# Hybrid encoder trunk on one core: low-part score matmul over 128 rows with zero-padded key tiles, five temporaries in place of six

## The chip, the cores and the metric

The kernel runs on one core of a Trainium2 chip. The time is the device time of one execution, in microseconds (us), and a kernel's figure is the median of its runs. TensorE does the matmuls (PE; its weight loads are PEld), VectorE (DVE), ScalarE (ACT) and GpSimd (POOL) the elementwise work, and SyncE (SP) issues most of the DMAs.

## The reference, cut to what matters

Two layers work on one sequence of 512 tokens with 1024 channels, all in float32. Each layer is half a SwiGLU step, four attention mixers side by side with four heads of 64 channels each, a projection back, another half SwiGLU step and a gate; an RMSNorm stands before each. The mixers are a neighbourhood attention (NA), a sliding window (SWA), a dilated window (DIL) and a latent one (MLA).

```python
for i in range(DEPTH):
    x = x + 0.5 * swiglu(rms_norm(x, ffn1_norm[i]), ffn1_w_gate[i], ffn1_w_up[i], ffn1_w_down[i])
    z = rms_norm(x, mix_norm[i]) @ w_in[i]
    z_na, z_swa, z_dil, z_mla = jnp.split(z, IN_SPLITS, axis=-1)
    y = jnp.concatenate([rms_norm(y_m, group_norm[i, m]) for the four mixers], axis=-1)
    x = x + y @ w_out[i]
    x = x + 0.5 * swiglu(rms_norm(x, ffn2_norm[i]), ffn2_w_gate[i], ffn2_w_up[i], ffn2_w_down[i])
    gate = jax.nn.sigmoid(rms_norm(x, ple_norm[i]) @ ple_w_gate[i])
    x = x + gate * (p[i] @ ple_w_proj[i])
return rms_norm(x, final_norm)
# in every mixer, for one head and a block of 128 queries:
#   s = q @ k.T * scale (+ bias, or masked);  o = softmax(s) @ v
```

## The kernel before, in words

**Products of two parts.** Activations lie in SBUF with channels on the 128 partitions and the 512 tokens in the free dimension. A float32 operand is kept as a high part (its rounding to the matmul's format) and a low part (what is left), and a product is three matmuls: high by high, high by low, low by high. For the projections these are L200, L201 and L202 in `mm3y`, each 128 rows by 512 columns. The weights come in by DMA (`pieces`, L157 to L175): a tile of raw weights lands, ScalarE rounds it into `wh`, and VectorE subtracts to make `wl` (GpSimd does it in the attention part, where `mixing` is set).

**Keys and queries.** Two heads share a tile: the first has rows 0 to 63, the second 64 to 127. `stack` (L333 to L350) prepares such a tile for the score product. Of the keys it makes a tile `t` with one half for each head, in which the head's 64 rows hold the high part and the other 64 rows a copy of it, and a tile `kl` [128, 512] whose rows hold the low parts of both heads, each in its own 64 rows (L341 to L343; the tag `kl` has two buffers). Of the queries it makes one tile with a half for each head: the head's own rows hold the high part, the other 64 rows the low part. So one matmul of 128 rows (L397) gives high by high plus low by high, and a second one (L398) over the head's 64 rows alone adds high by low:

```python
nc.tensor.matmul(s, lhsT=q[:, e, qs], rhs=k[0][:, e, k0:k1], start=True, stop=False)
nc.tensor.matmul(s, lhsT=q[rows, e, qs], rhs=k[1][rows, k0:k1], start=False, stop=True)
```

This holds for NA, SWA and DIL. The latent heads have 96 channels, and `rows` is None there: three matmuls of 128 rows (L392 to L394).

**One head.** `qk` runs for four blocks of 128 queries. A block's scores `s` have 256 or 384 columns where the window is a band, 512 otherwise. L404 on VectorE adds the mask and takes the minimum (or L401 without a mask), ScalarE takes the exponential into a tile `P` (L410; eight buffers). `tr` transposes P on TensorE (L439, into a score bank), ScalarE and VectorE split it into `PT` (L442, L443), and `pv` multiplies it with the values (L455, twice for each block, high and low); L463 adds two halves of that bank. After each second head `pair_end` spreads the softmax factors by transposes (L469). `value` scales a projection (L363 or, permuted, L361) and transposes it later (L368).

**The order of the work.** In `mix` a loop goes over 16 heads and six steps for each; at a step it issues score, transpose and pv work of the heads that are under way, and then `pump` issues a share of the projections of the later heads, so that TensorE has work while the other engines do the softmax. TensorE's instructions and SP's DMAs run in the order in which the program is written. The order on VectorE, ScalarE and GpSimd comes from the framework's scheduler, which also hands out the buffers. `mix` starts with the NA heads, then SWA, the latent ones, DIL.

**Temporaries.** `tmp` (L56) is a ring of six tiles of 128x512 float32. It serves the rotation (L326, L328, L330), the sums of squares (L215 on ScalarE, L216 on GpSimd), the gate blocks of the feed-forward part (`gated`, two tiles for each of the 88 blocks: L273 empties the gate bank into one, tanh goes to the other, L276 and L277 multiply, L120 makes the split), and the latent heads (`d_lat`, `d_kpe`, `d_up`). At the start of the latent heads `d_lstat` makes the factor `rkv` of the latent's norm, in a tile of its own (L558, by `rspread`, L239), and `d_up` uses it for keys (L586) and values (L363); a copy of the rotary key goes into each latent key tile (a DMA issued by GpSimd), after the split of the rotary key (L122 and L120).

`setup_mix` (L98) loads the masks for the attention part; it is called in the first feed-forward part.

Of the kernel before, what the change touches and what calls it, by code (L numbers as in the profile page):

```python
# [9 lines left out]
F32 = mybir.dt.float32  # L10
F32R = mybir.dt.float32r
AF = mybir.ActivationFunctionType
ALU = mybir.AluOpType
# [4 lines left out]
T = 512  # L18
# [16 lines left out]
class Encoder:  # L35
# [18 lines left out]
        return self.sb.tile(shape, dt, tag=tag, name=self.nm(tag), bufs=bufs)  # L54

    def tmp(self):  # L56
        return self.tile("tmp", [128, T], F32, 6)

    def act(self):
        return self.tile(self.tags[0], [128, 2, T], F32R, 8)  # L60
# [37 lines left out]
    def setup_mix(self):  # L98
        nc, a, c = self.nc, self.a, self.const
        self.sink = c.tile([128, self.depth, 4], F32, name="sink")  # L100
        nc.sync.dma_start(self.sink, a["sink"])
        self.nsink = c.tile([128, self.depth, 4], F32, name="nsink")
        nc.gpsimd.tensor_scalar(out=self.nsink, in0=self.sink, scalar1=-1.0, scalar2=None, op0=ALU.mult)
        self.na_mask = c.tile([128, 7, 16], F32, name="na_mask")
        nc.sync.dma_start(self.na_mask, a["na_mask"])
        self.swa_mask = c.tile([128, 384], F32, name="swa_mask")
        nc.sync.dma_start(self.swa_mask, a["swa_mask"])
        self.dil_mask = c.tile([128, 896], F32, name="dil_mask")
        nc.sync.dma_start(self.dil_mask, a["dil_mask"])

    def g(self, l, off, k):
        c = l * GAINS + off + k
        return self.gain[:, c:c + 1]
# [122 lines left out]
            nc.tensor.transpose(bc[:, t * 128:(t + 1) * 128], rc[:, t:t + 1].to_broadcast([128, 128]), self.ident)  # L236
        return bc

    def rspread(self, rc, tag="rb"):  # L239
        nc = self.nc  # L240
        bc = self.spread(rc)
        rb = self.tile(tag, [128, T], F32, 1)
        nc.scalar.activation(rb, bc, AF.Copy)
        return rb

# [87 lines left out]
    def stack(self, u, scale):  # L333
        nc = self.nc
        t = self.big()
        lo, up = slice(0, 64), slice(64, 128)
        if scale is None:
            for e, r, w in ((0, lo, up), (1, up, lo)):
                nc.scalar.activation(t[r, e], u[r], AF.Copy)
                nc.vector.tensor_copy(t[w, e], t[r, e].bitcast(F32))  # L340
            kl = self.tile("kl", [128, T], F32R, 2)  # L341
            for e, r in ((0, lo), (1, up)):
                nc.vector.tensor_tensor(out=kl[r], in0=u[r], in1=t[r, e].bitcast(F32), op=ALU.subtract)  # L343
            return t, kl
        for e, r in ((0, lo), (1, up)):
            nc.scalar.activation(t[r, e], u[r], AF.Copy, scale=scale)
        for e, r, w in ((0, lo, up), (1, up, lo)):
            nc.vector.scalar_tensor_tensor(out=t[w, e], in0=u[r], scalar=scale, in1=t[r, e].bitcast(F32),
                                           op0=ALU.mult, op1=ALU.subtract)
        return t  # L350
# [28 lines left out]
    def qk(self, st, t):  # L379
        nc, h = self.nc, st  # L380
        band, mask, sink = h["band"], h["mask"], h["sink"]
        if t == 0:
            h["ne"] = self.tile("ne", [128, 4], F32, 3)
            h["P"], h["k0"] = [], []
        q, k, rows, ne = h["q"], h["k"], h["rows"], h["ne"]
        k0 = 128 * max(0, t - 1) if band else 0
        k1 = 128 * min(4, t + 2) if band else T
        w = k1 - k0
        s = self.small()[:, :w]
        qs = slice(t * 128, (t + 1) * 128)  # L390
        if rows is None:
            nc.tensor.matmul(s, lhsT=q[:, 0, qs], rhs=k[:, 0, k0:k1], start=True, stop=False)  # L392
            nc.tensor.matmul(s, lhsT=q[:, 0, qs], rhs=k[:, 1, k0:k1], start=False, stop=False)
            nc.tensor.matmul(s, lhsT=q[:, 1, qs], rhs=k[:, 0, k0:k1], start=False, stop=True)  # L394
        else:
            e = h["odd"]
            nc.tensor.matmul(s, lhsT=q[:, e, qs], rhs=k[0][:, e, k0:k1], start=True, stop=False)  # L397
            nc.tensor.matmul(s, lhsT=q[rows, e, qs], rhs=k[1][rows, k0:k1], start=False, stop=True)  # L398
        p = self.tile("P", [128, T], F32, 8)
        if mask is None:  # L400
            nc.vector.tensor_reduce(ne[:, t:t + 1], s, AX.X, ALU.min)  # L401
            src = s
        else:
            nc.vector.tensor_tensor_reduce(  # L404
                out=p[:, :w], in0=s, in1=mask(t), scale=1.0,
                scalar=3e38 if sink is None else sink[0], op0=ALU.add, op1=ALU.min,
                accum_out=ne[:, t:t + 1])
            src = p[:, :w]
        ls = h["l8"][:, h["odd"]]
        nc.scalar.activation(p[:, :w], src, AF.Exp, bias=ne[:, t:t + 1], scale=-1.0,  # L410
                             accum_out=ls[:, t:t + 1])
        h["P"].append(p)
        h["k0"].append(k0)
        if t == 3:
            if sink is not None:
                se = self.tile("se", [128, 4], F32, 2)
                nc.scalar.activation(se, ne, AF.Exp, bias=sink[1])
                nc.vector.tensor_tensor(ls, ls, se, op=ALU.add)
            if h["odd"]:
                rl = self.tile("rl", [128, 2, 4], F32, 2)  # L420
                nc.vector.reciprocal(rl, h["l8"])
                rx = self.tmp()
                nc.scalar.activation(rx.rearrange("p (t e d) -> p t e d", t=4, e=2),
                                     rl.rearrange("p e t -> p t e").unsqueeze(3).to_broadcast([128, 4, 2, 64]),
                                     AF.Copy)
                h["rx"] = rx
# [125 lines left out]
    def d_lstat(self):  # L552
        nc, a = self.nc, self.a
        yield

        def finish():
            r = self.rspread(self.t["rq"], "rg")
            self.rkv = self.rspread(self.t["rkv"], "rkv")  # L558
            t = self.tile("nb", [128, 896], F32, 1)[:, :T]
            nc.sync.dma_start(t, a["mlaq"])  # L560
            nc.gpsimd.tensor_tensor(out=t, in0=t, in1=r, op=ALU.mult)
            self.mlaq = t

        self.later.append([7, finish, "lstat"])
        return True
# [414 lines left out]
```

## Time and profile before

| | |
|---|---|
| runs | 2168.96 us median of 3 (2166.63, 2168.96, 2170.75) |
| profiled execution: span | 2163.3 us; no whole time of its own is given, so the median stands 5.66 us above this span |
| TensorE busy | 2117.2 us, 98% (9564 matmuls); weight loads 1718.6 us |
| VectorE busy | 1210.5 us, 56% |
| ScalarE busy | 930.1 us, 43% |
| GpSimd busy | 280.0 us, 13% |
| mean granted clock of TensorE | 0.994 of full speed |

The span is the time from the profiled execution's first to its last instruction. Busy time is the sum over an engine's instructions, overlaps taken once; a matmul's row begins before the one ahead of it is through, so the durations of neighbouring rows add up to more than the time they take, and the step from one start to the next is what one costs. A wait is an idle stretch, with the instruction that ended it. The two layers take turns with two tile tags (`act` and `big`): what is named big in the first layer is named act in the second, so the same line has two groups. The attention part of the first layer lies between 395 and 640 us, that of the second between about 1460 and 1705.

### The profile page before, as it was taken

Reading aid. Unit: us, or ns where it says so; the run is one execution under the profiler, and the core shown is the slowest. Engines: PE = TensorE matmul, PEld = TensorE weight load, DVE = VectorE, ACT = ScalarE, POOL = GpSimd, SP = SyncE. Lnnn points to the kernel's source line nnn. Section 1 sums busy time; section 2 is a strip of 40 time slices with the busy share of each in tenths; the row PEclk is TensorE's granted clock in tenths of the full one; section 3 lists DMA queues with packets and bytes.
Section 4 is the critical chain, followed back from the end, with each engine's and each line's share of the span. In section 5 each row is a group of like instructions: output and inputs, shape, how many; then the busy total and the mean of one; then the engine's idle time right before and its main releaser. Section 6 shows DMA issues by size and latency. Waiting matters only on the chain.

```text
span 2163.3 us, 25721 instructions
## 1 busy us (share of the span) xinstructions
PE 2117.2 (98%) x9564; PEld 1718.6 (79%) x9564; DVE 1210.5 (56%) x1926; ACT 930.1 (43%) x1690; POOL 280.0 (13%) x230
## 2 busy tenths in 40 slices
PE   8999999999999999999999999999999999999997
PEld 6888888677778888888888888886777788888886
DVE  5444446567766444456654444555687654444554
ACT  4332334477754332333533233345677533233343
POOL 2000001444321000001100000025332200000011
PEclk9999999999999999999999999999999999999998
DMA  3232223212112222223322322232121122322322
GB/s 129 97 109 99 98 94 111 90 60 75 40 54 93 98 96 99 98 98 96 100 96 98 94 102 98 93 102 93 64 59 49 59 98 98 94 101 98 102 92 89
DMA packets 63358, 195.38 MB, mean 90 GB/s; under 512 B 7552, under 2 KB 15872, under 8 KB 63232
## 3 DMA queue, kind: packets, MB, share of 16 engines
q1 hardware_dynamic: 61808, 187.92, 26.0%
q0 software_dynamic: 1280, 5.77, 1.0%
q8 instruction: 75, 1.23, 0.2%
q14 instruction: 51, 0.42, 0.1%
q10 hardware_dynamic: 144, 0.05, 0.0%
HBM read 189.51 MB, written 2.10 MB: 89 GB/s over the span
## 4 chain that ended last, share of the span: by engine, by line
PE 92%; DVE 4%; ACT 2%; issue 1%; DMA 1%; POOL 0%; POOLq 0%; SPq 0%; DVEq 0%; ACTq 0%
PE ps L200 15%; PE ps L201 15%; PE ps L202 15%; PE s L201 13%; PE s L200 13%; PE s L202 13%; PE pv L455 2%; PE s L439 2%; PE s L398 2%; PE s L397 1%; DVE kl L343 1%; PE s L225 1%; PE s L236 0%; ACT tmp L326 0%; DVE PT L443 0%
## 5 line engine op out<-in xcount | busy, mean ns | idle before, releaser
L173 ACT ACTIVATE wh<-raw 128x512 fp32r<-128x512 f32 (+1 forms) x712 | 437.8, 615 | 971.2 <-PE ps L201 457.3
L175 DVE TENSOR_TENSOR wl<-raw,wh 128x512 fp32r<-128x512 f32 (+1 forms) x614 | 435.6, 710 | 405.6 <-ACT wh L173 399.0
L200 PE MATMUL ps<-act,wh 128*128 128x512 f32 x616 | 248.8, 404 | 6.1 <-ACT act L122 6.1
L216 POOL TENSOR_TENSOR acc<-acc,tmp 128x512 f32<-128x512 f32 x54 | 72.3, 1340 | 1365.4 <-ACT tmp L215 1365.0
L200 PE MATMUL ps<-big,wh 128*128 128x512 f32 x616 | 247.0, 401 | 0.0
L201 PE MATMUL ps<-act,wh 128*128 128x512 f32 x616 | 242.7, 394 | 3.3 <-DVE act L123 3.1
L202 PE MATMUL ps<-act,wl 128*128 128x512 f32 x616 | 242.1, 393 | 0.0
L202 PE MATMUL ps<-big,wl 128*128 128x512 f32 x616 | 240.6, 391 | 0.0
L201 PE MATMUL ps<-big,wh 128*128 128x512 f32 x616 | 240.3, 390 | 0.0
L200 PE MATMUL s<-act,wh 128*128 128x512 f32 x520 | 202.4, 389 | 0.0
L200 PE MATMUL s<-big,wh 128*128 128x512 f32 x520 | 202.4, 389 | 0.0
L202 PE MATMUL s<-act,wl 128*128 128x512 f32 x520 | 202.3, 389 | 0.0
L202 PE MATMUL s<-big,wl 128*128 128x512 f32 x520 | 202.3, 389 | 0.0
L201 PE MATMUL s<-big,wh 128*128 128x512 f32 x520 | 202.3, 389 | 0.0
L201 PE MATMUL s<-act,wh 128*128 128x512 f32 x520 | 202.3, 389 | 0.0
L175 POOL TENSOR_TENSOR wl<-raw,wh 128x512 fp32r<-128x512 f32 (+1 forms) x98 | 127.4, 1300 | 286.6 <-ACT wh L173 286.4
L200 PEld LDWEIGHTS ps<-act,wh 128*128 128x128 f32 x616 | 116.7, 189 | 30.1 <-ACT act L122 6.4
L201 PEld LDWEIGHTS ps<-act,wh 128*128 128x128 f32 x616 | 116.7, 189 | 28.5 <-DVE act L123 7.3
L202 PEld LDWEIGHTS ps<-act,wl 128*128 128x128 f32 x616 | 116.6, 189 | 24.6
L202 PEld LDWEIGHTS ps<-big,wl 128*128 128x128 f32 x616 | 115.7, 188 | 24.7
L200 PEld LDWEIGHTS ps<-big,wh 128*128 128x128 f32 x616 | 116.0, 188 | 23.5 <-issue 1.1
L201 PEld LDWEIGHTS ps<-big,wh 128*128 128x128 f32 x616 | 116.2, 189 | 21.4
(172 smaller groups left out, 3373.1 us busy)
## 6 DMA issues: line engine op xcount, KB each, us to landing
raw<-in_ffn_gu SPq DMA_DIRECT2D x175, 512.0 KB, 3.5
raw<-in_ffn_d SPq DMA_DIRECT2D x64, 512.0 KB, 3.4
raw<-in_w_in SPq DMA_DIRECT2D x40, 512.0 KB, 3.5
raw<-in_ffn_d SPq DMA_DIRECT2D x64, 192.0 KB, 2.5
raw<-in_w_out SPq DMA_DIRECT2D x16, 512.0 KB, 3.5
raw<-in_ple SPq DMA_DIRECT2D x16, 384.0 KB, 3.0
raw<-in_ple SPq DMA_DIRECT2D x16, 256.0 KB, 2.6
nb<-in_na_bias POOLq DMA_DIRECT2D x8, 448.0 KB, 4.1
```

The lines of the kernel that those rows point to most:

```text
L173: nc.scalar.activation(hi, r, AF.Copy)
L175: eng.tensor_tensor(out=lo, in0=r, in1=hi.bitcast(F32), op=ALU.subtract)
L200: nc.tensor.matmul(ps, lhsT=wh[:, k], rhs=x[:, 0], start=start and k == 0, stop=False)
L201: nc.tensor.matmul(ps, lhsT=wh[:, k], rhs=x[:, 1], start=False, stop=False)
L202: nc.tensor.matmul(ps, lhsT=wl[:, k], rhs=x[:, 0], start=False, stop=stop and k == last)
L216: eng.tensor_tensor(out=acc, in0=acc, in1=sq, op=ALU.add)
L225: nc.tensor.matmul(ss[:, t:t + 1], lhsT=acc[:, t * 128:(t + 1) * 128], rhs=self.ones, start=True, stop=True)
L343: nc.vector.tensor_tensor(out=kl[r], in0=u[r], in1=t[r, e].bitcast(F32), op=ALU.subtract)
L397: nc.tensor.matmul(s, lhsT=q[:, e, qs], rhs=k[0][:, e, k0:k1], start=True, stop=False)
L398: nc.tensor.matmul(s, lhsT=q[rows, e, qs], rhs=k[1][rows, k0:k1], start=False, stop=True)
L439: nc.tensor.transpose(tp[:, t * 128:(t + 1) * 128], h["P"][t][:, o:o + 128], self.ident)
L455: nc.tensor.matmul(pv[:, c], lhsT=vb, rhs=h["pt"][b][:, i, c], start=b == 0 and i == 0, stop=b == 3 and i == 1, skip_group_check=True)
```

## The change

The low part of a key tile gets a tile of its own shape, `klz` [128, 2, 512], with a half for each head: the head's 64 rows hold its low part, the other 64 rows are zero. There are two such tiles, made once in `setup_mix` and taken in turn (`nkl`); four memsets on GpSimd clear the rows that stay zero, and L343 writes only the others. The second score matmul then takes all 128 rows of both operands: the other 64 rows of the query tile, its low part, meet zeros. To make room, `tmp` has five buffers and not six, the tag `kl` is gone, and `rkv` takes one of the eight buffers of the tag `P`.

```diff
--- before.py
+++ after.py
@@ -54,7 +54,7 @@
         return self.sb.tile(shape, dt, tag=tag, name=self.nm(tag), bufs=bufs)
 
     def tmp(self):
-        return self.tile("tmp", [128, T], F32, 6)
+        return self.tile("tmp", [128, T], F32, 5)
 
     def act(self):
         return self.tile(self.tags[0], [128, 2, T], F32R, 8)
@@ -107,6 +107,11 @@
         nc.sync.dma_start(self.swa_mask, a["swa_mask"])
         self.dil_mask = c.tile([128, 896], F32, name="dil_mask")
         nc.sync.dma_start(self.dil_mask, a["dil_mask"])
+        self.klz = [c.tile([128, 2, T], F32R, name=f"klz{i}") for i in range(2)]
+        self.nkl = 0
+        for t in self.klz:
+            nc.gpsimd.memset(t[64:128, 0].bitcast(F32), 0.0)
+            nc.gpsimd.memset(t[0:64, 1].bitcast(F32), 0.0)
 
     def g(self, l, off, k):
         c = l * GAINS + off + k
@@ -236,10 +241,10 @@
             nc.tensor.transpose(bc[:, t * 128:(t + 1) * 128], rc[:, t:t + 1].to_broadcast([128, 128]), self.ident)
         return bc
 
-    def rspread(self, rc, tag="rb"):
+    def rspread(self, rc, tag="rb", bufs=1):
         nc = self.nc
         bc = self.spread(rc)
-        rb = self.tile(tag, [128, T], F32, 1)
+        rb = self.tile(tag, [128, T], F32, bufs)
         nc.scalar.activation(rb, bc, AF.Copy)
         return rb
 
@@ -338,9 +343,10 @@
             for e, r, w in ((0, lo, up), (1, up, lo)):
                 nc.scalar.activation(t[r, e], u[r], AF.Copy)
                 nc.vector.tensor_copy(t[w, e], t[r, e].bitcast(F32))
-            kl = self.tile("kl", [128, T], F32R, 2)
+            kl = self.klz[self.nkl % 2]
+            self.nkl += 1
             for e, r in ((0, lo), (1, up)):
-                nc.vector.tensor_tensor(out=kl[r], in0=u[r], in1=t[r, e].bitcast(F32), op=ALU.subtract)
+                nc.vector.tensor_tensor(out=kl[r, e], in0=u[r], in1=t[r, e].bitcast(F32), op=ALU.subtract)
             return t, kl
         for e, r in ((0, lo), (1, up)):
             nc.scalar.activation(t[r, e], u[r], AF.Copy, scale=scale)
@@ -395,7 +401,7 @@
         else:
             e = h["odd"]
             nc.tensor.matmul(s, lhsT=q[:, e, qs], rhs=k[0][:, e, k0:k1], start=True, stop=False)
-            nc.tensor.matmul(s, lhsT=q[rows, e, qs], rhs=k[1][rows, k0:k1], start=False, stop=True)
+            nc.tensor.matmul(s, lhsT=q[:, e, qs], rhs=k[1][:, e, k0:k1], start=False, stop=True)
         p = self.tile("P", [128, T], F32, 8)
         if mask is None:
             nc.vector.tensor_reduce(ne[:, t:t + 1], s, AX.X, ALU.min)
@@ -555,7 +561,7 @@
 
         def finish():
             r = self.rspread(self.t["rq"], "rg")
-            self.rkv = self.rspread(self.t["rkv"], "rkv")
+            self.rkv = self.rspread(self.t["rkv"], "P", 8)
             t = self.tile("nb", [128, 896], F32, 1)[:, :T]
             nc.sync.dma_start(t, a["mlaq"])
             nc.gpsimd.tensor_tensor(out=t, in0=t, in1=r, op=ALU.mult)
```

TensorE's and SP's instructions keep their order. On VectorE the order changes at the start of the latent heads. Before, the values' scaling (L363, into tmp_4105) stands between the low parts of the first two latent queries (L123, into big_4062 and big_4076); `ps` are projection banks, `nb` and `rkv` factors:

```order
L586 TENSOR_TENSOR tmp_4095<-ps_4085,rkv_4004 64x512
L123 SCALAR_TENSOR_TENSOR big_4062<-tmp_4060,big_4062 128x512
L363 TENSOR_TENSOR tmp_4105<-ps_4101,rkv_4004 128x512
L123 SCALAR_TENSOR_TENSOR big_4076<-tmp_4074,big_4076 128x512
L120 TENSOR_TENSOR big_4091<-tmp_4089,big_4091 64x512
L577 TENSOR_TENSOR tmp_4118<-ps_4111,nb_4006 128x512
L120 TENSOR_TENSOR big_4097<-tmp_4095,big_4097 64x512
```

In the changed kernel, whose lines have other numbers (L363 is L369, L123 is L128, L120 is L125):

```order
L592 TENSOR_TENSOR tmp_4098<-ps_4088,P_4007 64x512
L128 SCALAR_TENSOR_TENSOR big_4065<-tmp_4063,big_4065 128x512
L128 SCALAR_TENSOR_TENSOR big_4079<-tmp_4077,big_4079 128x512
L125 TENSOR_TENSOR big_4094<-tmp_4092,big_4094 64x512
L369 TENSOR_TENSOR tmp_4108<-ps_4104,P_4007 128x512
L125 TENSOR_TENSOR big_4100<-tmp_4098,big_4100 64x512
L583 TENSOR_TENSOR tmp_4121<-ps_4114,nb_4009 128x512
```

The values' scaling stands two instructions later, behind the second query's low part and the first latent key's, and the third query's scaling (L583) one later too.

On GpSimd the four clears stand at the program's start. Before, around the identity matrix:

```order
masks.py:197 MEMSET ident 128x128
L96 MEMSET nhalf 128x4
masks.py:199 ISA
masks.py:199 AFFINE_SELECT ident<-ident 128x128
L216 TENSOR_TENSOR acc_102<-acc_102,tmp_174 128x512
```

In the changed kernel:

```order
masks.py:197 MEMSET ident 128x128
L96 MEMSET nhalf 128x4
L113 MEMSET klz_1043 64x512
L114 MEMSET klz_1043 64x512
masks.py:199 ISA
masks.py:199 AFFINE_SELECT ident<-ident 128x128
L113 MEMSET klz_1044 64x512
L114 MEMSET klz_1044 64x512
L221 TENSOR_TENSOR acc_102<-acc_102,tmp_174 128x512
```

Two of them come ahead of the identity matrix's second step, two behind it, and all four ahead of the first addition of squares.

## Rows read from the trace of the kernel before

**Rows 1.** The chain of work that ended last, share of the span by engine.

```profile
PE 92%; DVE 4%; ACT 2%; issue 1%; DMA 1%; POOL 0%; POOLq 0%; SPq 0%; DVEq 0%; ACTq 0%
```

**Rows 2.** Three stretches: us; busy PE, PEld, DVE, ACT, POOL; PEclk; DMA share; GB/s.

```profile
395.00:430.00 35.00, 31.23 (x126) 22.46 (x127) 17.18 (x40) 15.66 (x37) 16.23 (x13) 0.90 0.26 96
408.00:512.00 104.00, 101.75 (x499) 78.50 (x499) 70.64 (x158) 72.52 (x170) 48.56 (x39) 1.00 0.20 68
680.00:1055.00 375.00, 375.00 (x1661) 310.60 (x1661) 193.39 (x289) 132.10 (x217) 11.41 (x9) 1.00 0.29 97
```

**Rows 3.** Timeline of TensorE: start, duration, line, tiles; 256 columns, projection behind.

```profile
407.60 0.28 PE L397 MATMUL s<-big,big 128*128 128x256 f32 x1
407.80 0.38 PE L398 MATMUL s<-kl,big 64*128 64x256 f32 x1
408.12 0.50 PE L200 MATMUL ps<-act,wh 128*128 128x512 f32 x1
408.45 0.40 PE L201 MATMUL ps<-act,wh 128*128 128x512 f32 x1
```

**Rows 4.** Timeline of TensorE: 512 columns, four transposes behind.

```profile
571.37 0.39 PE L397 MATMUL s<-big,big 128*128 128x512 f32 x1
571.68 0.50 PE L398 MATMUL s<-kl,big 64*128 64x512 f32 x1
572.11 0.66 PE L439 MATMUL s<-ident,P 128*128 128x128 f32 x4
572.53 0.47 PE L200 MATMUL ps<-act,wh 128*128 128x512 f32 x1
```

**Rows 5.** Timeline of TensorE: 128-row matmuls and transposes back to back.

```profile
440.25 0.40 PE L455 MATMUL pv<-PT,big 128*128 128x256 f32 x2
440.48 0.60 PE L469 MATMUL s<-ident,tmp 128*128 128x128 f32 x4
440.84 0.36 PE L397 MATMUL s<-big,big 128*128 128x256 f32 x1
```

**Rows 6.** TensorE's waits from 395 to 640: total us, times, longest.

```profile
PE s L368 <- DVE tmp L361: 3.0, 1, 3.0
PE s L397 <- DVE ne L404: 2.3, 2, 1.4
PE s L392 <- ACT big L122: 1.5, 1, 1.5
PE s L368 <- DVE tmp L363: 1.3, 1, 1.3
```

**Rows 7.** L398: count, min/median/max ns, forms; last row: idle before it, us, times.

```profile
L398 PE MATMUL s<-kl,big x48: 379/439/687, 399.4 to 621.8; 64*128 64x256 f32 x16, 64*128 64x384 f32 x16, 64*128 64x512 f32 x16
...
L398 PE MATMUL s<-kl,act x48: 379/439/579, 1466.5 to 1687.0; 64*128 64x256 f32 x16, 64*128 64x384 f32 x16, 64*128 64x512 f32 x16
...
  issue: 26.0, 82
```

**Rows 8.** Timeline of VectorE from 436.8 to 446.4: start, duration, line, tiles.

```profile
436.83 0.69 DVE L328 TENSOR_TENSOR tmp<-ps,tab 128x512 f32<-128x512 f32 x1 [1.86 <-ACT tmp L326]
...
440.91 2.50 DVE L343 TENSOR_TENSOR kl<-tmp,big 64x512 fp32r<-64x512 f32 x1
...
446.30 0.42 DVE L404 CUSTOM_DVE_ANT_0 P<-s,nb 128x256 f32<-128x256 f32 x1
```

**Rows 9.** Timelines of TensorE and of VectorE around 469.9.

```profile
469.91 0.61 PE L455 MATMUL pv<-PT,big 128*128 128x256 f32 x2
...
469.65 0.43 DVE L443 TENSOR_TENSOR PT<-s,PT 128x256 fp32r<-128x256 f32 x1
```

**Rows 10.** Timeline of VectorE in the feed-forward part: one gate block.

```profile
30.27 0.69 DVE L273 TENSOR_TENSOR tmp<-ps,rb 128x512 f32<-128x512 f32 x1
...
34.80 0.68 DVE L120 TENSOR_TENSOR big<-tmp,big 128x512 fp32r<-128x512 f32 x1
```

**Rows 11.** Timeline of GpSimd: its first additions, and the idle time before.

```profile
8.21 9.77 POOL L216 TENSOR_TENSOR acc<-acc,tmp 128x512 f32<-128x512 f32 x6 [6.89 <-ACT tmp L215]
```

## The prediction

> **What bounds the kernel now.** I read the chain that ended last first, then the busy times by stretch, then TensorE's rows one by one around the changed instruction, and last the waits of TensorE and what its releasers did. The chain is TensorE for 92% of the span [rows 1]. The stretches say where that is strict: in the feed-forward part TensorE is busy 375.00 of 375.00 us with VectorE at 193.39, and in an attention stretch it is busy 101.75 of 104.00 with VectorE at 70.64 and ScalarE at 72.52 [rows 2]. So an instruction that TensorE gets rid of in the attention part shortens the run, until another engine's chain ends later. A busy TensorE row overlaps the next, so I count the steps from one start to the next and not the durations.
>
> **The low-part pass.** For each score block TensorE runs two matmuls: L397 with 128 rows, then L398 with 64 rows. There are 96 of the second kind, 48 in each layer (the second layer's tiles have the names act, the first's big), a third each with 256, 384 and 512 columns [rows 7]. What a 64-row matmul costs is read from its neighbours' starts.
>
> - 256 columns, a projection matmul behind it [rows 3]: L397 at 407.60, L398 at 407.80, L200 at 408.12, L201 at 408.45: steps of 0.20, 0.32 and 0.33, 0.85 in all. Without the 64-row form: two 128-row matmuls of 256 columns take 0.23 together (440.25 to 440.48 [rows 5]), and a 512-column step is 0.23 (375.00 us over 1661 matmuls, nearly all of that size [rows 2]). That makes 0.46. Excess 0.39.
> - 512 columns, four transposes behind it [rows 4]: L397 at 571.37, L398 at 571.68, the transposes at 572.11, the next matmul at 572.53, 1.16 in all. Without: two steps of 0.23, and four transposes up to the next matmul 0.36 (440.48 to 440.84 [rows 5]): 0.82. Excess 0.34.
>
> The excess has three parts: some 0.1 ahead of the 64-row matmul, 0.2 behind it, and 0.05 to 0.1 at the next one. This is what an array looks like that empties when its shape changes and empties again when it changes back. The weight loads agree: their part of the engine stood idle 26.0 us before L398, 82 times, for no releaser that the profile shows [rows 7]. In the changed kernel L398 has the shape of L397, so I take the 128-row steps for it, and all three parts go. The followers, counted along TensorE's rows: 52 of the 96 pairs are followed by a projection matmul or by the second product (pv), 44 by transposes; the 384-column pairs, of which no row stands here, are put with their follower. Sum: 52 x 0.39 + 44 x 0.34 = 20.3 + 15.0 = **35.2 us**. The bounds of this term are 0, if the gap doesn't belong to the row count, and 36.5, with 0.40 and 0.355 as the rows' rounding allows.
>
> The Trainium skill has a rule that speaks against this term: the page "TensorE: Matmul & The Clock Gate", in the table of "Why this matters for your kernels", says that one matmul of few rows takes as long as one with all 128, and that fewer rows gain only by running several side by side. By it alone the two forms would cost the same, and the term would be 0. The rows show 0.32 behind a 64-row matmul of 256 columns where 128 rows take 0.115 [rows 3, 5], so here the measurement decides, and the other page, "TensorEngine Tiling (Array Packing)", "Key Properties", would explain it: a change of tiling mode drains the engine. It gives no figure.
>
> **What eats into it.** Where TensorE waits for a chain that began at a projection's end, the pairs in between no longer cover that chain, and their saving turns into a longer wait. TensorE's score matmuls waited for VectorE's L404 twice in the first layer, 2.3 us [rows 6]. Of the later place the rows show the cause: L328 takes a projection at 436.83, the split of the key tile follows, L343 takes 2.50, and L404 comes only at 446.30 [rows 8]. Between lie two pairs, so 0.39 + 0.34 = 0.73 of saving is lost; the earlier place is alike. At the start of the latent heads TensorE waits 1.3 us for L363 and then 1.5 more at L392 [rows 6], for a chain that begins with the rotary key's projection; the last pair's tail (0.2 + 0.1) lies behind that projection and is lost. Per layer 2 x 0.73 + 0.3 = 1.76, in two layers 3.5. Then there are places where the second product starts right behind VectorE's subtraction: the pair L455 that begins at 469.91 needs the one that ran from 469.65 to 470.08 [rows 9]. I count four in the first layer and charge half of a pair's excess, 0.2, to each: 8 x 0.2 = 1.6. Together **5.1 us** lost. Lower bound 3.5; upper bound half of the term, 17.6, if VectorE and ScalarE, at some 70% in this stretch [rows 2] and in strict order, can't follow any faster.
>
> **The order on VectorE at the latent heads** changes, since with five temporaries the values' L363 must wait for the slot that the first query's split frees. L363 comes two operations later, 2 x 0.68 with the duration of L120 [rows 10], so the transposes behind it start some 1.3 later. I cost this at nothing: the 1.5 wait at L392 that follows is for the rotary key's copy, and it shrinks by as much. If that cover is gone, it is 1.3 in each layer, 2.6.
>
> **Five temporaries elsewhere: nothing.** In the gate stage a block takes two slots, and the first block's lived from 30.27 to 35.48 [rows 10], while a block's two projections are 48 matmuls of 0.23, 11 us: a slot comes round after some 27. TensorE has no idle there to show a shortage [rows 2]. Where the sums of squares go to GpSimd, six adds took 9.77 us [rows 11], 1.6 each, and one lands for every 2.7 us or more of TensorE's work. The kv factor in place of a probability tile leaves seven of eight; it is done with before the second latent head asks for its last.
>
> **Four clears on GpSimd** stand ahead of its first add. That engine was idle 6.89 us there [rows 11]. No row prices a clear of 64x512; it lies between nothing and one of those adds, 1.6, so four take at most 6.5 and are hidden. Cost 0, bounds 0 and 0. The writes to the key tile's low part keep their count, engine and size; only the column half differs.
>
> **Sum.** 35.2 - 5.1 = 30.1 us off. The profiled span is 2163.3, so 2133.2. The runs' median is 5.7 above that span, which I keep as what lies around it: 2168.96 - 30.1 = **2138.9 us**.
>
> **Rivals.**
>
> - *Half is lost.* VectorE's and ScalarE's queues set the pace once TensorE is faster. For: both at 70%, chains like that of rows 8. Against: TensorE's waits in 245 us of attention are few, 2.3 + 1.3 + 1.5 among them [rows 6]. 17.6 off: 2151.4. The clock belongs here: it was granted at 0.90 of full speed in the stretch 395 to 430, full speed being 2.4 GHz and the lower level 1.2, which cost some 3.5 us there [rows 2]; TensorE had idled 3.0 us for L361 before it [rows 6]. If the wait for L363 grows to 2.6 and brings another such spell in each layer, it takes 7 of the 30: 2146. Chance 0.20 for the two.
> - *All of it and more.* The longer waits don't appear, and the low-clock spells shrink: 35.2 + 3.5 off, 2130.3. Chance 0.10.
> - *No gain.* By the rule above, or since the gap belongs to the change of the moving tile and not of the rows. Against the second: L397's own tile also differs from that of the projection before it, and there the step is the usual one. What is left is 0 to 2.6 of the new order: 2169 to 2171.6. Chance 0.05.
> - *Slower: the five slots run out in the feed-forward part.* Place: L273, which empties a gate result, waits for a slot, and TensorE behind it for the bank. Price: if each of the 88 gate blocks came one VectorE pass (0.69) late, 60.7 us, less the 30.1: 2199.6. It decides from the point at which a slot's life passes the 27 us of the round; it was 5.2 [rows 10]. Chance 0.02.
>
> **How the numbers follow.** The forecast, with 25 to 35 us off, has 0.63. A measurement of this kernel can tell about 0.2%, 4.3 us, from no change; the first three cases are all beyond it. Faster 0.63 + 0.20 + 0.10 = 0.93, same 0.05, slower 0.02. The range reaches to the low end of the third case, 2131, and over the half-lost case to 2153; it leaves out some 0.1.
>
> **What would show it.** Right: L398 with 128 rows follows L397 by 0.115, 0.175 and 0.23 and is followed after as much; the idle of its weight loads is gone; the score matmuls' wait for VectorE goes from 2.3 to near 4 in a layer, that for L363 from 1.3 to 2.6, with the wait at L392 shorter by the difference; the feed-forward stretch keeps its length. Wrong: steps of 0.32 or more behind L398; new waits of TensorE over 10 us in a layer; gaps in the feed-forward part; a clock below 1.00 in the attention stretches.

## The result, and the profile after

The changed kernel took 2145.38 us (median of 4 runs, 2143.31 to 2146.03) where the kernel before took 2168.26 (4 runs, 2166.63 to 2170.75): ratio 0.9893, 95% interval 0.9879 to 0.9907, 22.9 us off. The time lies in the stated range, 6.5 above the forecast of 2138.9 and beside the 2146 that the first rival gave for spells of low clock. The profiled executions have spans of 2163.3 and 2143.0, 20.3 apart. In the runs that list both, the time is 1.8 above the span; for the kernel before the median stood 5.7 above the profiled span, so that execution was one of its quickest.

In the changed kernel lines have other numbers: the two score matmuls are L403 and L404 (before L397 and L398), the projections L205 to L207 (L200 to L202), the transposes L445 (L439), pv L461 (L455), the mask and minimum L410 (L404), the key's copies L345 (L340) and low part L349 (L343), the values' scalings L367 and L369 (L361, L363) and their transposes L374 (L368), the latent score L398 (L392), the split of the transposed P L449 (L443), the exponential L416 (L410), the mask's bias L651 (L645), the weights' high and low parts L178 and L180 (L173, L175).

The chain that ended last, where [rows 1] stood, and three stretches with the columns of [rows 2]:

```profile
PE 91%; DVE 5%; ACT 2%; issue 1%; DMA 1%; POOL 0%; SPq 0%; POOLq 0%; DVEq 0%; ACTq 0%
```

```profile
395.00:430.00 35.00, 29.40 (x134) 24.62 (x135) 19.52 (x42) 16.73 (x40) 16.77 (x13) 0.90 0.26 94
405.00:506.00 101.00, 94.96 (x500) 80.15 (x499) 71.96 (x158) 73.20 (x171) 49.72 (x39) 0.97 0.21 70
680.00:1055.00 375.00, 375.00 (x1662) 310.62 (x1661) 193.49 (x288) 132.90 (x218) 12.78 (x11) 1.00 0.30 97
```

The feed-forward stretch is as it was. The attention stretch takes 101 us for the work of 104, and TensorE, busy 101.75 before, is busy 94.96 now, at a clock of 0.97 where it was 1.00. The pairs themselves, on TensorE's timeline, where [rows 3] and [rows 4] stood:

```profile
408.44 0.28 PE L403 MATMUL s<-big,big 128*128 128x256 f32 x1
408.55 0.28 PE L404 MATMUL s<-klz,big 128*128 128x256 f32 x1
408.67 0.40 PE L205 MATMUL ps<-act,wh 128*128 128x512 f32 x1
408.90 0.40 PE L206 MATMUL ps<-act,wh 128*128 128x512 f32 x1
...
566.26 0.39 PE L403 MATMUL s<-big,big 128*128 128x512 f32 x1
566.49 0.39 PE L404 MATMUL s<-klz,big 128*128 128x512 f32 x1
566.72 0.60 PE L445 MATMUL s<-ident,P 128*128 128x128 f32 x4
567.07 0.48 PE L205 MATMUL ps<-act,wh 128*128 128x512 f32 x1
```

Steps of 0.11, 0.12 and 0.23, 0.46 in all where it was 0.85; and 0.81 up to the projection behind the transposes where it was 1.16. The saving at a pair is what the sum took. What ate into it stands in TensorE's waits over the whole run (total us, times, longest), before:

```profile
PE s L397 <- DVE ne L404: 4.7, 4, 1.4
...
PE s L368 <- DVE tmp L363: 2.7, 2, 1.3
PE s L392 <- DMA act<-kpe: 1.9, 1, 1.9
PE pv L455 <- DVE PT L443: 1.9, 6, 0.5
PE s L392 <- ACT big L122: 1.5, 1, 1.5
```

and after:

```profile
PE s L403 <- DVE ne L410: 10.7, 4, 3.4
...
PE s L374 <- DVE tmp L369: 3.9, 2, 2.0
PE pv L461 <- DVE PT L449: 3.5, 10, 0.7
...
PE s L398 <- DMA big<-kpe: 1.0, 1, 1.0
PE s L398 <- ACT tmp L468: 0.7, 1, 0.7
```

The waits for L410, L369 and L449 grew by 6.0, 1.2 and 1.6; that of the latent scores shrank from 3.4 to 1.7: net 7.1. With the smaller ones, all of TensorE's waits in the two attention parts (395 to 640 and 1440 to 1720) grew by 6.5, from 22.0 to 28.5. So of 35.2 some 28.7 are left; 20.3 were measured. Most of the other 8.4 lies in the clock. Behind the longer waits TensorE's steps double for a while; on its timeline, behind the wait that ended at 444.72 (column in brackets: idle time before, and what ended it):

```profile
444.72 0.44 PE L403 MATMUL s<-big,big 128*128 128x384 f32 x1 [2.15 <-DVE ne L410]
...
446.12 0.63 PE L206 MATMUL ps<-act,wh 128*128 128x512 f32 x1
446.55 0.63 PE L207 MATMUL ps<-act,wl 128*128 128x512 f32 x1
```

A step of 0.43 where it is 0.23 otherwise; from 436 to 450 the granted clock was 0.88. The stretches behind the three lengthened waits of the first layer, columns as in [rows 2]:

```profile
414.00:424.00 10.00, 7.01 (x30) 5.72 (x29) 6.71 (x16) 4.83 (x13) 2.19 (x4) 0.83 0.29 98
436.00:450.00 14.00, 11.70 (x54) 9.43 (x54) 12.46 (x22) 10.64 (x23) 8.62 (x6) 0.88 0.15 47
506.00:516.00 10.00, 7.05 (x28) 5.35 (x27) 7.59 (x13) 4.51 (x10) 2.15 (x3) 0.83 0.43 95
```

Each lost 1.7 us to the clock (10 us at 0.83, 14 at 0.88). The attention parts of the changed kernel's profiled execution have seven such spells: one behind each of the six lengthened waits (for L410 twice and for L369, in each layer) and one behind the first layer's wait for L367. In the profiled execution of before no stretch behind a wait for L404 or L363 had one; its attention parts lost 5.1, all of it behind the two waits for L361 (15 us at 0.77 and 10 at 0.83). That is 6.8 more for the changed kernel. With the 6.5 of the waits it leaves 21.9 of the 35.2; the last 1.6 down to 20.3 no row places.

### The profile page after: what moved, and what is told of

It is laid out like the page before. It is cut to its first block, busy times and chain, and to the rows that moved or that the text cites. A ratio compares the mean times of both kernels' runs of the same rounds, so it can differ in the third digit from the quotient of the medians.

```text
span 2143.0 us, 25740 instructions
## 1 busy us (share of the span) xinstructions
PE 2091.5 (98%) x9564; PEld 1726.3 (81%) x9564; DVE 1210.1 (56%) x1926; ACT 929.2 (43%) x1690; POOL 283.3 (13%) x234
## 4 chain that ended last, share of the span: by engine, by line
PE 91%; DVE 5%; ACT 2%; issue 1%; DMA 1%; POOL 0%; SPq 0%; POOLq 0%; DVEq 0%; ACTq 0%
PE ps L205 15%; PE ps L206 15%; PE ps L207 15%; PE s L207 13%; PE s L205 13%; PE s L206 13%; PE pv L461 2%; PE s L445 2%; PE s L403 1%; DVE klz L349 1%; PE s L404 1%; ACT tmp L331 1%; PE s L230 1%; DVE PT L449 1%; ACT PT L448 0%
## 5 line engine op out<-in xcount | busy, mean ns | idle before, releaser
L178 ACT ACTIVATE wh<-raw 128x512 fp32r<-128x512 f32 (+1 forms) x712 | 437.7, 615 | 959.4 <-PE ps L206 440.7
L180 DVE TENSOR_TENSOR wl<-raw,wh 128x512 fp32r<-128x512 f32 (+1 forms) x614 | 435.4, 709 | 405.8 <-ACT wh L178 399.4
L205 PE MATMUL ps<-act,wh 128*128 128x512 f32 x616 | 248.5, 403 | 5.9 <-ACT act L127 5.9
L205 PE MATMUL ps<-big,wh 128*128 128x512 f32 x616 | 246.3, 400 | 0.0
L207 PE MATMUL ps<-act,wl 128*128 128x512 f32 x616 | 243.1, 395 | 0.0
L207 PE MATMUL ps<-big,wl 128*128 128x512 f32 x616 | 241.0, 391 | 0.0
L205 PE MATMUL s<-big,wh 128*128 128x512 f32 x520 | 202.4, 389 | 0.0
L205 PE MATMUL s<-act,wh 128*128 128x512 f32 x520 | 202.4, 389 | 0.0
L207 PE MATMUL s<-act,wl 128*128 128x512 f32 x520 | 202.3, 389 | 0.0
L207 PE MATMUL s<-big,wl 128*128 128x512 f32 x520 | 202.3, 389 | 0.0
L180 POOL TENSOR_TENSOR wl<-raw,wh 128x512 fp32r<-128x512 f32 (+1 forms) x98 | 128.0, 1306 | 265.2 <-ACT wh L178 259.5
L205 PEld LDWEIGHTS ps<-act,wh 128*128 128x128 f32 x616 | 117.5, 191 | 27.6 <-ACT act L127 6.0
L207 PEld LDWEIGHTS ps<-act,wl 128*128 128x128 f32 x616 | 117.5, 191 | 24.7
L207 PEld LDWEIGHTS ps<-big,wl 128*128 128x128 f32 x616 | 116.2, 189 | 24.9
L205 PEld LDWEIGHTS ps<-big,wh 128*128 128x128 f32 x616 | 116.3, 189 | 21.3
```

The costliest lines, as they stand in the source:

```text
L178: nc.scalar.activation(hi, r, AF.Copy)
L180: eng.tensor_tensor(out=lo, in0=r, in1=hi.bitcast(F32), op=ALU.subtract)
L205: nc.tensor.matmul(ps, lhsT=wh[:, k], rhs=x[:, 0], start=start and k == 0, stop=False)
L207: nc.tensor.matmul(ps, lhsT=wl[:, k], rhs=x[:, 0], start=False, stop=stop and k == last)
```

## The experiments

Ratios are to the kernel before, run on the same chip.

**Is it the row count?** The changed kernel with 64 rows again:

```diff
-            nc.tensor.matmul(s, lhsT=q[:, e, qs], rhs=k[1][:, e, k0:k1], start=False, stop=True)
+            nc.tensor.matmul(s, lhsT=q[rows, e, qs], rhs=k[1][rows, e, k0:k1], start=False, stop=True)
```

> The changed kernel with one thing undone: the low-part matmul takes 64 rows again, of the new tiles; five temporaries and the clears stay. Theory (the gain is the row count's): the steps of before return, 0.3 behind a 64-row matmul of 256 columns, and the time with them: 2166 to 2172. Rival (the gain comes from the new tile or the ring): it stays at about 2145, with steps of 0.115 to 0.23 behind L404.

2168.72, ratio 1.0005 (0.9996 to 1.0014). Everything else of the change stayed in, and the gain was gone: it is the row count's.

**Does the ring cost anything?** The kernel before with five temporaries and the kv factor in tag P:

```diff
-        return self.tile("tmp", [128, T], F32, 6)
+        return self.tile("tmp", [128, T], F32, 5)
...
-            self.rkv = self.rspread(self.t["rkv"], "rkv")
+            self.rkv = self.rspread(self.t["rkv"], "P", 8)
```

> The kernel before with five temporaries and the kv factor in a probability tile, and nothing else. Theory (costed at nothing): 2166 to 2171, the wait for the values' L363 longer by 1.3 in each layer and the one at L392 shorter by as much; a spell of low clock behind it would add 1.7 in each. Rival (the ring takes what the change gained less than forecast): 2173 to 2178.

2167.02, ratio 0.9998 (0.9989 to 1.0007): nothing. TensorE's waits from 395 to 640:

```profile
PE s L368 <- DVE tmp L363: 2.5, 1, 2.5
...
PE s L392 <- DMA big<-kpe: 0.6, 1, 0.6
```

The one wait grew by 1.2, the other shrank by 0.9 [rows 6], as the new order on VectorE let expect.

**What does a 64-row matmul cost?** The kernel before with the second matmul twice:

```diff
+            nc.tensor.matmul(s, lhsT=q[rows, e, qs], rhs=k[1][rows, k0:k1], start=False, stop=False)
             nc.tensor.matmul(s, lhsT=q[rows, e, qs], rhs=k[1][rows, k0:k1], start=False, stop=True)
```

> The kernel before with the 64-row low-part matmul issued twice in a row, so the scores hold the low part twice. Theory (the price belongs to the change of shape, paid once on the way in and once on the way out): the second one adds a bare step, 0.115, 0.175 or 0.23, 96 times, 16.6 us, of which waits may swallow a fifth: 2181 to 2185. Rival (every 64-row matmul pays 0.2 or more above its step): 96 x (0.17 + 0.2) = 36 us, 2200 or more.

2183.94, ratio 1.0075 (1.0061 to 1.0089), 16 us more for 96 more matmuls: the bare steps. From the first score matmul to the second projection behind it the steps now add up to 0.97 (406.52 to 407.49) where they were 0.85 [rows 3]. The timelines of the weight loads and of TensorE show where the price sits (L399 is the second of the two):

```profile
406.28 0.19 PEld L397 LDWEIGHTS s<-big,big 128*128 128x128 f32 x1
406.72 0.18 PEld L398 LDWEIGHTS s<-kl,big 64*128 64x128 f32 x1 [0.25 <-issue]
406.83 0.19 PEld L399 LDWEIGHTS s<-kl,big 64*128 64x128 f32 x1
407.15 0.19 PEld L200 LDWEIGHTS ps<-act,wh 128*128 128x128 f32 x1
```

```profile
406.52 0.28 PE L397 MATMUL s<-big,big 128*128 128x256 f32 x1
406.72 0.38 PE L398 MATMUL s<-kl,big 64*128 64x256 f32 x1
406.95 0.28 PE L399 MATMUL s<-kl,big 64*128 64x256 f32 x1
407.15 0.49 PE L200 MATMUL ps<-act,wh 128*128 128x512 f32 x1
407.49 0.39 PE L201 MATMUL ps<-act,wh 128*128 128x512 f32 x1
```

Between equal shapes the next weights load ahead of their matmul: those of L397 at 406.28 for 406.52, those of L399 at 406.83 for 406.95. Where the shape changes, into 64 rows (406.72) and out of it (407.15), load and matmul begin together: the load no longer hides under the matmul ahead. That is paid once on the way in and once on the way out, for one 64-row matmul and for two in a row alike. So both pages of the Trainium skill hold that the prediction weighed. By its "TensorE: Matmul & The Clock Gate", table of "Why this matters for your kernels", a matmul of few rows takes as long as one of all 128, and a second 64-row matmul does cost the step of a 128-row one. By its "TensorEngine Tiling (Array Packing)", "Key Properties", a change of tiling mode drains the engine, and here a trip into 64 rows and back costs 0.34 to 0.39.

**Where did a third of it go?** First the clock: matmuls by a tile of zeros ahead of the two waits for L410 in each layer (places and counts found from the trace), accumulating into the projection bank in progress:

```diff
+FILL = {(1, 3): 12, (3, 2): 8}
...
+                    self.fill(FILL.get((n, b), 0))
                     self.qk(h, b)
...
+    def fill(self, n):
+        for _ in range(n):
+            self.nc.tensor.matmul(self.cur, lhsT=self.zero, rhs=self.xs[0][:, 0], start=False, stop=False)
```

> The changed kernel with matmuls by a tile of zeros, which add nothing, into the projection bank in progress, ahead of the two score matmuls of each layer that wait for L410: 12 at the first place, 8 at the second, 2.8 and 1.8 us of work inside waits of 3 and 2. Theory (the longer waits cost twice, since the clock falls to its lower level behind each, 3.4 us at half speed): no such spell at these four places, 4 x 1.7 = 6.8 us off the changed kernel: 2137 to 2140. Rival (the clock falls for another reason, or the spell costs nothing): 2144 to 2147; if the matmuls push what comes behind them, up to 2150.

2142.1, ratio 0.9883 (0.987 to 0.9897): 2 to 3 us of the 6.8 forecast, and not told apart from the change's 0.9893. The slow steps behind the four waits were gone. Of the spells at the other two places (L367, L369), in the profiled execution one was twice as long, one came that the change's execution lacked, and one of the change's was missing. So the same was done at all four places of a layer where TensorE waits 2 us or more, beside the changed kernel on the same chip:

```diff
+FILLV = {"nv0": 12, "mv0": 8}
...
         def finish():
+            self.fill(FILLV.get(key, 0))
             p = self.small()
```

> The changed kernel itself once more, on the chip of the next run, so that the two can be compared: 2143 to 2147.

> As the first run with zero matmuls, and such matmuls also at the two other places of each layer where TensorE waits 2 us or more: 12 ahead of the transposes that wait for the first values (L367), 8 ahead of those that wait for the latent values (L369). Theory (each such wait brings, in most executions, a spell at the lower clock of 3.4 us, worth 1.7): no spell in the attention parts, a granted clock of 1.00 there in every stretch, 7 to 11 us off the changed kernel, 2134 to 2138. Rival (the clock falls for another reason, or costs nothing): spells remain, 2142 to 2147.

The changed kernel: 2145.84, ratio 0.9898 (0.9882 to 0.9915). With zeros at four places: 2136.25, ratio 0.9856 (0.9842 to 0.9871). 9.6 us come back from work that computes nothing. Stretches of it, columns as in [rows 2]:

```profile
395.00:430.00 35.00, 34.66 (x178) 29.21 (x177) 18.70 (x47) 19.74 (x47) 18.43 (x15) 1.00 0.32 109
436.00:450.00 14.00, 13.24 (x66) 10.44 (x65) 11.81 (x23) 10.38 (x23) 6.23 (x5) 1.00 0.14 52
```

The clock is 1.00 in both, where it was 0.90 and 0.88. Not all of the 9.6 is the change's loss: the kernel before had spells behind its waits for L361 too [rows 2].

**Why did the waits grow?** At the later place of a layer by 0.8 (1.38 to 2.15), the two pairs of the forecast; at the earlier one from 0.87 to 2.99. VectorE's timeline there, before:

```profile
415.72 1.35 DVE L340 CAST big<-big 64x512 fp32r<-64x512 f32 x1
417.08 0.68 DVE L343 TENSOR_TENSOR kl<-tmp,big 64x512 fp32r<-64x512 f32 x1
417.78 0.42 DVE L340 CAST big<-big 64x512 fp32r<-64x512 f32 x1
418.21 0.69 DVE L343 TENSOR_TENSOR kl<-tmp,big 64x512 fp32r<-64x512 f32 x1
418.93 0.42 DVE L404 CUSTOM_DVE_ANT_0 P<-s,nb 128x256 f32<-128x256 f32 x1
```

after, and GpSimd beside it:

```profile
411.76 1.17 DVE L345 CAST big<-big 64x512 fp32r<-64x512 f32 x1
412.94 1.68 DVE L349 TENSOR_TENSOR klz<-tmp,big 64x512 fp32r<-64x512 f32 x1
414.64 0.42 DVE L345 CAST big<-big 64x512 fp32r<-64x512 f32 x1
415.07 1.66 DVE L349 TENSOR_TENSOR klz<-tmp,big 64x512 fp32r<-64x512 f32 x1
416.76 0.42 DVE L410 CUSTOM_DVE_ANT_0 P<-s,nb 128x256 f32<-128x256 f32 x1
...
412.59 1.49 POOL L180 TENSOR_TENSOR wl<-raw,wh 128x512 fp32r<-128x512 f32 x1
414.83 1.35 POOL L180 TENSOR_TENSOR wl<-raw,wh 128x512 fp32r<-128x512 f32 x1 [0.75 <-ACT wh L178]
```

The preparation of a key takes 5.00 in place of 3.21. Each low part that runs beside a weight's low part on GpSimd takes 1.0 more: TensorE, quicker, took its weights earlier, and GpSimd's work on the next ones moved onto VectorE's. ScalarE's timeline shows it by when the next weight is rounded, before and after:

```profile
418.41 0.63 ACT L173 ACTIVATE wh<-raw 128x512 fp32r<-128x512 f32 x1 [0.72 <-PE ps L201]
...
414.12 0.63 ACT L178 ACTIVATE wh<-raw 128x512 fp32r<-128x512 f32 x1 [0.73 <-POOL wl L180]
```

Before, it waits for TensorE and comes at the end of the key's preparation; after, it waits for GpSimd and comes in the middle, and GpSimd's work on it (414.83) falls on the second low part. The test is to take GpSimd's weights away:

```diff
-                eng = nc.gpsimd if self.mixing else nc.vector
+                eng = nc.vector
```

> The changed kernel with the weights' low parts made by VectorE in the attention part too, as elsewhere, so that GpSimd has only the rotation and the bias there. Theory (VectorE's key operations stretch by the time that GpSimd works beside them): at the first place L345 takes 0.42 and L349 0.69 each time, and the wait for L410 there falls from 3.0 to about 1; VectorE has some 49 operations of 0.69 more in each layer, so the whole may still end anywhere between 2138 and 2155. Rival (the stretch comes from elsewhere): L345 and L349 still take 1.2 and 1.7 there.

2128.82, ratio 0.9821 (0.9807 to 0.9834), below the 2138 to 2155 that the theory allowed: VectorE does more and is done earlier. All of L345 and L349 in the first layer (count, min/median/max ns):

```profile
L345 DVE CAST big<-big x10: 420/422/423, 392.1 to 583.2; 64x512 fp32r<-64x512 f32 x10
...
L349 DVE TENSOR_TENSOR klz<-tmp,big x10: 682/686/2512, 392.5 to 583.7; 64x512 fp32r<-64x512 f32 x10
```

No copy is stretched any more, and most low parts take 0.69. The one of 2.51 began at 432.45, beside the bias that GpSimd still subtracts (L651, 432.28 to 434.41). The wait for L410 has left TensorE's list, and the score matmuls wait 4.6 in the whole run for L479 instead, another step of VectorE. The Trainium skill, "GPSIMD Engine Reference", "8. Key points", says that GpSimd shares its SBUF interfaces with VectorE and contends with VectorE instructions that have two inputs in SBUF or run in a two-port mode. The trace agrees for the low parts, which have two inputs (0.69 alone, 1.68 beside GpSimd); the copies have one, and whether they run in such a mode no run here shows.

**Can the chain be shortened?** The key's copies on ScalarE, from the source:

```diff
-                nc.vector.tensor_copy(t[w, e], t[r, e].bitcast(F32))
+                nc.scalar.activation(t[w, e], u[r], AF.Copy)
```

> The changed kernel with the two copies of a key's high part (L345) made by ScalarE from the source instead of by VectorE. Theory (what was lost is VectorE's key preparation, which stands ahead of L410 in its strict order, stretched where it overlaps GpSimd): 1.6 to 2.2 us leave that chain at each of the four places, the score matmuls' wait for L410 falls from 10.7 to 4 or less, and the spells of low clock behind it go: 5 to 10 us off the changed kernel, 2135 to 2140. Rival (ScalarE, as busy as VectorE there, takes over as the late one): waits for L416 and L448 instead, 2144 to 2150.

2125.3, ratio 0.9802 (0.9789 to 0.9816): 20 us below the change, twice what was expected, and no version was faster. TensorE's waits over the whole run:

```profile
PE pv L461 <- DVE PT L449: 5.2, 11, 0.9
...
PE s L403 <- DVE ne L410: 2.8, 2, 1.5
```

The wait for L410 falls from 10.7 to 2.8. The waits for L367 (6.0 before and after the change, 3.0 in each layer) have left the list too, which I had not counted: the first values' scaling stood behind the first key's preparation (L367 began at 396.86 after the change, at 393.25 in this run), and in the first layer the low clock came behind it.

Two versions with the low part on GpSimd, with the copies on ScalarE and without:

```diff
-                nc.vector.tensor_tensor(out=kl[r, e], in0=u[r], in1=t[r, e].bitcast(F32), op=ALU.subtract)
+                nc.gpsimd.tensor_tensor(out=kl[r, e], in0=u[r], in1=t[r, e].bitcast(F32), op=ALU.subtract)
```

> The copies on ScalarE as in the run before, and the key's low part (L349) on GpSimd, so that VectorE prepares no keys at all. Theory: the wait for L410 falls under 1 us in all, 2133 to 2138, and L349 takes some 1.3 us each on GpSimd. Rival (GpSimd's queue makes the weights' low parts late, and L207 waits): 2142 to 2150.

> The changed kernel with only the key's low part (L349) on GpSimd; the copies (L345) stay on VectorE. Theory: VectorE's chain loses two operations, 1.4 us without and up to 3.4 with overlap, but the copies overlap GpSimd's added work and stretch: wait for L410 between 3 and 6 instead of 10.7, 2137 to 2142. Rival as above: 2142 to 2150.

2133.88 and 2133.36, ratio 0.984 for both (0.9827 to 0.9854 and to 0.9853). Better than the change, worse than the copies on ScalarE alone. With both moves TensorE's transposes still wait 4.9 for L410, not under 1. GpSimd's queue is late, though not at the weights: L410 waits for the mask's bias, which GpSimd subtracts at L651 behind the keys. On VectorE's timeline:

```profile
413.71 0.42 DVE L410 CUSTOM_DVE_ANT_0 P<-s,nb 128x256 f32<-128x256 f32 x1 [2.66 <-POOL nb L651]
```

Over all heads of the neighbourhood attention VectorE stood idle 20.4 ahead of L410, 12.0 of it for L651; with the copies on ScalarE alone 11.9 and 10.4. So the bias is late there too, and it doesn't by itself make the 8 us between these versions. The clock has a part in it: with both moves the waits for L410 are 2.4 and 2.6 long, and the attention parts of the profiled execution have four stretches of 10 us at 0.83, behind these waits and those for L369; with the copies alone the waits are 1.5 and 1.3, and there is one such stretch. That makes 5.1, where the two spans are 6.6 apart; no run takes this share by itself.

**What is the row count worth then?** The copies on ScalarE with 64 rows (the edits of the first run and of the one on copies), and the copies with the weights on VectorE (the edits of the two):

> The key copies on ScalarE, and the low-part matmul over 64 rows again, of the new tiles: against the run with the copies alone it prices the row count where VectorE's key preparation no longer makes TensorE wait. Theory (what the change lost of its 35 us, it lost to those waits and the clock behind them): the row count is worth 30 to 35 there, 2155 to 2160. Rival (a third of it is lost whatever VectorE does, as in the change): 2147 to 2150.

> The key copies on ScalarE and the weights' low parts on VectorE in the attention part, both in the changed kernel. Theory (both shorten the same chain, the keys' preparation ahead of L410, so they don't add up): 2122 to 2129. Rival (they act at different places): 2108 to 2116.

2151.56, ratio 0.993 (0.9917 to 0.9942), against 0.9802 with 128 rows: 0.0128, 27.8 us. That is more than the change's 22.9 and less than the 30 to 35 I expected (the time lies between the two forecasts): in the 64-row run TensorE never waits for L410 long enough to be listed, and 2.4 for L449, in the 128-row run 3.9 (2.8 at L403, 1.1 at L445) and 5.2. So some 7 us of the 35 go to VectorE's latency even then, and 27.8 and 7 together come near the 35.2 of the sum. The other: 2125.57, ratio 0.9811 (0.9798 to 0.9824), the same as the copies alone. Both shorten the same chain, and don't add up.

## Why the prediction was right or wrong

- **The price of the low-part pass** was right, term and reason. 0.39 and 0.35 off a pair, as the rows after show; back with 64 rows and only with them; a price of the change of shape, since the second 64-row matmul adds a bare step. (The sum for its upper bound, 36.5, comes to 36.4.)
- **The ring, the clears, the feed-forward part** cost nothing, as costed. A clear took 0.52, four of them 2.1 of the idle time ahead of the first addition, which begins at 7.62 where it began at 8.21 [rows 11]. Alone the ring has a ratio of 0.9998. The waits of the latent heads moved the way that was told.
- **What eats into it** was mis-sized: 5.1 forecast, 7.1 measured. Its step on pv was right (1.6 forecast, 1.6 measured in total, at ten waits where there were six), that of the latent heads too cautious (0.6 lost forecast, the waits for L369 and at L398 together shorter by 0.5). The step that failed is "the earlier place is alike": 2 x 0.73 in a layer forecast, 3.0 measured (6.0 in two). I took the chain behind the projection as fixed in length. It isn't: at the earlier place the key's preparation grew by 1.8, since GpSimd's weights moved onto it; from the scaling that opens the chain to L410 it is 1.45 (413.88 to 418.93 before, 410.26 to 416.76 after), which with the 0.7 of the two pairs makes the 2.1 by which the wait grew. The rows that show it in the kernel before, a copy of 1.35 and one of 0.42, were there to be read; L343's 2.50 in [rows 8] is the same thing.
- **The clock** stood in a rival and not in the sum. I had put one more spell in each layer, behind the wait for L363; there came one behind each lengthened wait, three in a layer. In the runs, filling these waits and those for L367 gave 9.6 back. By its size (7 us and 2146; 6.8 by the clock rows) this rival came true, by its place only in part.
- **What lies around the span** was 5.7 in the sum and is 1.8. The other 3.9 was that the profiled execution ran quicker than the median: runs of before went from 2163.99 to 2171.75, from a mean clock of 0.995 to one of 0.989. By spans the forecast missed by 9.8 (2133.2 against 2143.0), by medians by 6.5.

Left open: the 1.6 us of the saving that neither the listed waits nor the clock account for; why one wait of 2.9 us (for L367, in the changed kernel's second layer) was followed by no spell; and whether moving the bias of L651 would let the versions with GpSimd's keys gain more, which was not tried.

## What to carry to other kernels

A matmul of few rows (here 64) among full ones pays for the change of shape on the way in and on the way out; zeros in the rest of the rows were cheaper here, and a second 64-row matmul right behind the first paid its step alone. What a bound engine saves is kept only where its feeders have slack: list its waits, take the saving between a wait's start and the event that ends it as lost, and count with a spell of low clock behind each wait that the saving stretches (here behind all six). And look for the next wait in the feeder's own order: two copies moved from VectorE to ScalarE were worth nearly as much as the change.

## What the runs showed of the hardware that was not expected

- A weight load does not run ahead of its matmul across a change between 128 and 64 rows; load and matmul begin together (406.72, 407.15).
- A 64x512 operation of VectorE within SBUF grows by nearly the time that a subtraction on GpSimd runs beside it: copies from 0.42 to 1.17, low parts from 0.69 to 1.68 and 2.50 (the one of 1.68 had GpSimd beside it for 1.14 and took 0.99 longer).
- Matmuls by zeros in waits of 2 to 3 us kept TensorE's granted clock at 1.00, which is 2.4 GHz, through both attention parts, and gave 9.6 us back in all.
- In the changed kernel's profiled execution seven of the eight waits of 2.0 to 3.4 us in the attention parts were followed by a spell at the lower level, 1.2 GHz, of 1.7 us lost each.
